# Attention logits in a one-core decoder layer: three 64-row products per half become two 128-row products, with q stacked, k doubled and padded, and three bias bands kept on chip

## The chip, the cores and the metric

The kernel runs on one core of a Trainium2 chip. The metric is device time in microseconds (us) of one execution; the median of three runs is the figure compared. The core has a matrix engine (PE, whose weight loads are listed apart as PEld), a vector engine (DVE), a scalar engine (ACT), a general engine (POOL) that also issues transfers, and a queue engine (SP) that only issues transfers.

## The reference, cut to what matters

One decoder layer over 512 tokens of width 1024, in float32. After a normalisation and one wide projection, 8 heads of differential attention run beside a recurrent branch; the two are gated, merged and followed by a squared-ReLU MLP. The part the change touches is the attention's logits:

```python
q = rmsnorm(q, q_g)                      # per head and half: 64 values
k = rmsnorm(k, k_g)
...
bias = jnp.transpose(bias_tab[rel_bucket(rel)], (2, 0, 1))
logits = jnp.einsum('bqhcd,bkhcd->bhcqk', q_blk, k) * scale   # c = 0, 1: two halves of 64
logits = logits + bias[None, :, None]
logits = jnp.where(rel >= 0, logits, -jnp.inf)
p = jax.nn.softmax(logits, axis=-1)
attn = p[:, :, 0] - lam * p[:, :, 1]
out = einsum(attn, v)
```

So each head has two logit matrices, each a product over 64 values, and the bias depends only on the head and on query minus key.

## The kernel before, in words

**Precision.** Matrix products run on a rounded float32 type. To keep accuracy each operand is split into a high part (rounded, made by ACT) and a low part (the remainder, made by DVE), and a product is three products: high by high, high by low, low by high (`mm3`, L136 to L139). Weights arrive as `wraw`, and are split into `whi` (ACT) and `wlo` (DVE), one unit of 128x1024 at a time.

**Stages.** From 0 to about 77 us the input is normalised and the first projections run. From 77 to about 283 us the attention runs; the rest of the layer follows.

**Attention.** It is one loop of 32 blocks. Block s is head s // 4 and query rows 128 * (s % 4). Per block: `logits` (PE, L563, six products of 64 rows, three for each half c; N = 256, 256, 384, 512 key columns for s % 4 = 0 to 3), `soft_a` (DVE adds the bias `toep` and takes the maximum, ACT takes the exponential), `soft_b` one step later (DVE normalises and combines the two halves; its last instruction is `pe<-pe,r`), `turn(s)` one more step later (PE transposes, L597, 128 columns each, s % 4 + 1 of them; then the split into `pt`), and `av` (PE). Between the blocks `fill_in` puts projection work for the next pair of heads on PE (products into `acc`), so that PE has something to do while the softmax of a block runs on DVE and ACT. Heads come in pairs; `qkv_pair(j)` computes q, k and v of heads 2j and 2j + 1 while pair j - 1 is in the attention loop. Its own `turn(qi, ...)` transposes q or k of one head (PE, L515, four transposes from `qn`), and `split` makes the high part (ACT, one instruction of 128x512) and the low part (DVE, one of 128x512) of `qkT`. There are 16 such turns: q and k of 8 heads.

**Bias.** `bias_table` makes for each head a 128x512 band `toep[h]` in SBUF, by two transfers on SP's queue; all eight bands have their own place.

**Order.** DVE, ACT and POOL keep the order of the program (`InOrder`). SP issues transfers in order. PE's attention instructions are placed by the compiling layer's scheduler, which may move a product past another one; its choice is fixed at build time, and the change shifts it.

Of the kernel before, what the change touches and what calls it, by code (L numbers as in the profile page):

```python
# [11 lines left out]
F32 = mybir.dt.float32  # L12
F32R = mybir.dt.float32r
I32 = mybir.dt.int32
AF = mybir.ActivationFunctionType
ALU = mybir.AluOpType
# [3 lines left out]
P = 128  # L20
S = 512
DM = 1024
NT = S // P
KT = DM // P
NH = 8
# [4 lines left out]
TW = 640  # L30
# [7 lines left out]
def tile_block(ctx: ExitStack, tc: tile.TileContext, x, w_in, w_rga, w_rgx, w_pa, w_pr, w_o,  # L38
               w_up, w_dn, rel_bias, smalls, lamv, onehot, out):
    nc = tc.nc  # L40
# [34 lines left out]
    V, A, G, T = InOrder(nc.vector), InOrder(nc.scalar), InOrder(nc.gpsimd), nc.tensor  # L75

    def psum(tag):
        return pp.tile([P, 512], F32, tag=tag, name=tag, bufs=nb[tag])
# [62 lines left out]
    def split(hi, lo, src, scale=None):  # L141
        if scale is None:
            A.copy(hi, src)
            V.tensor_tensor(out=lo, in0=src, in1=hi.bitcast(F32), op=ALU.subtract)
        else:
            A.activation(hi, src, AF.Copy, scale=scale)
            V.scalar_tensor_tensor(out=lo, in0=src, scalar=scale, in1=hi.bitcast(F32), op0=ALU.mult, op1=ALU.subtract)
# [65 lines left out]
    def rstd_of(dst, ss, n, width):  # L213
        t = sm.tile([P, width], F32, tag="ms", name="ms")
        V.tensor_scalar(out=t, in0=ss, scalar1=1.0 / n, scalar2=EPS, op0=ALU.mult, op1=ALU.add)
        G.tensor_tensor(out=dst, in0=t, in1=mhalf[:, :width], op=ALU.pow)
# [28 lines left out]
    def tok_proj(bank, ws, t):  # L245
        b = bank[:, 256 * (t % 2):256 * (t % 2) + 256]
        for k in range(KT):
            w = ws[k // 4]
            mm3(b, h_tok(k, t), (w[0][:, k % 4, :], w[1][:, k % 4, :]), k == 0, k == KT - 1)
            if t == NT - 1 and k % 4 == 3:  # L250
                wa.free()
        wa.pump()
# [42 lines left out]
    def unit(name, dt=F32R):  # L295
        return actp.tile([P, 2, S], dt, tag="unit", name=name)
# [11 lines left out]
    with tc.tile_pool(name="p1", bufs=1) as p1:  # L308
# [28 lines left out]
        ps = [[psum("at"), psum("at")] for z in range(2)]  # L337
        for k0, k1 in pieces:
            u, kk = k0 // 4, slice(k0 % 4, (k1 - 1) % 4 + 1)
# [64 lines left out]
    trep = [dp.tile([1, P * TW], F32, name=f"trep{h}", tag=f"trep{h}") for h in range(NH)]  # L404
# [3 lines left out]
    wk = es_at.enter_context(tc.tile_pool(name="wk", bufs=1, reuse_waits="tile"))  # L408
    t2 = {n: wk.tile([P, 2], F32, name=n) for n in ("ls", "le")}
    t8 = [wk.tile([P, KT], F32, name=n) for n in ("ab", "e", "den", "s", "s2", "po", "tmp", "mxl")]  # L410
    wk.tile([P, 32], F32, name="apart2")
    toep = [wk.tile([P, S], F32, tag=f"toep{h}", name=f"toep{h}") for h in range(NH)]
    PT = []
    for half in range(2):
        PT.append([wk.tile([P, 2 + 2 * half, 256], F32R, name=f"pt{half}{z}", tag=f"pt{half}{z}") for z in range(2)])
# [5 lines left out]
    def work(name):  # L421
        return wk.tile([P, S], F32, tag="pe", name=name, bufs=5)

    def bias_table():
        parts = ((0, 512), (512, 128))
        ohs = []
        for c0, n in parts:
            o = work("oh")
            nc.sync.dma_start(o[:64, :n], onehot[:, c0:c0 + n])
            ohs.append(o)  # L430
        rb = sm.tile([64, 32], F32, name="rbt", tag="rbt", bufs=1)
        G.memset(rb, 0.0)
        G.memset(rb[32:33, :], MASKED)
        nc.sync.dma_start(rb[0:NBUCKET, 0:NH], rel_bias)
        yield
        for (c0, n), o in zip(parts, ohs):
            ps = psum("at")
            T.matmul(ps[:32, :n], rb, o[:64, :n], start=True, stop=True)
            tb = work("tb")
            V.tensor_copy(tb[:32, :n], ps[:32, :n])  # L440
            nc.sync.dma_start(tdram[:, c0:c0 + n], tb[:NH, :n])
        yield
        for h in range(NH):
            nc.sync.dma_start(trep[h].rearrange("o (r y) -> o r y", r=P),
                              tdram[h:h + 1, :].rearrange("h (o y) -> h o y", o=1).broadcast_to([1, P, TW]))
            yield
            t0 = trep[h][0:1, :]
            nc.sync.dma_start(toep[h], bass.AP(tensor=t0.tensor, offset=t0.offset + 127, ap=[[TW - 1, P], [1, S]]))

    def lam_diff(lt):  # L450
        lv = lt[:, :256].rearrange("p (a b c) -> p a b c", a=2, b=2)
# [36 lines left out]
    def qkv_pair(j, qk, v):  # L488
        def proj(o, bank):
            ws = [wa.get(), wa.get()]  # L490
            for t in range(NT):
                if t % 2 == 0:
                    bank.append(psum("acc"))
                tok_proj(bank[t // 2], ws, t)
                yield 2.6

        def normed_a(b, qn):
            n = wk.tile([P, S], F32, tag="qn", name="qn", bufs=4)
            A.activation(n, b, AF.Square)
            ss = sm.tile([P, 8], F32, tag="ss8", name="ss8")  # L500
            V.tensor_reduce(out=ss, in_=n.rearrange("p (g d) -> p g d", g=8), axis=AX.X, op=ALU.add)
            rs = sm.tile([P, 8], F32, tag="rs8", name="rs8")
            rstd_of(rs, ss, 64, 8)
            qn.append(n)
            return b, n, rs

        def normed_b(b, n, rs):
            V.tensor_tensor(out=n.rearrange("p (g d) -> p g d", g=8), in0=b.rearrange("p (g d) -> p g d", g=8),
                            in1=rs.rearrange("p (g o) -> p g o", o=1).broadcast_to([P, 8, 64]), op=ALU.mult)

        def turn(qi, qn, gsc, hh):
            ps = psum("at")
            for t in range(NT):
                c0 = 256 * (t % 2) + P * hh
                T.transpose(out=ps[:, t * P:(t + 1) * P], in_=qn[t // 2][:, c0:c0 + P], identity=ident)  # L515
            d = unit("qkT")
            split(d[:, 0, :], d[:, 1, :], ps, gsc)
            qk[hh, qi] = d

        banks = {o: [] for o in (OQ, OK_, OV)}  # L520
        qn = {o: [] for o in (OQ, OK_)}
        pend, half = [], []
        for o, qi, gsc in ((OQ, 0, qg), (OK_, 1, kg), (OV, None, None)):
            for t, cost in enumerate(proj(o, banks[o])):
                half.append(None)
                ready = half.pop(0) if len(half) > 2 else None
                if ready:
                    normed_b(*ready)
                if t % 2 == 1:
                    b = banks[o][t // 2]  # L530
                    if o != OV:
                        half[-1] = normed_a(b, qn[o])
                    else:
                        vt = wk.tile([P, 2, 2, 256], F32R, tag="v", name="v", bufs=4)
                        split(vt[:, 0], vt[:, 1], b.rearrange("p (t c) -> p t c", t=2))
                        v.append(vt)
                if pend and t >= 2:
                    turn(*pend.pop(0))
                    cost += 0.45
                yield cost  # L540
                if j == 0 and o == OV and t == 0:
                    lam_diff(lt)
                if j == 0 and o != OQ:
                    next(bt)
            if o != OV:
                pend = [(qi, qn[o], gsc, 0), (qi, qn[o], gsc, 1)]

    def attention(fills, qks, vs, pads):
        st = {}

        def place(s):
            return s // NT, s % NT

        def logits(s):
            h, i = place(s)
            qk = qks[h // 2]
            qT, kT = qk[h % 2, 0], qk[h % 2, 1]
            N = max(256, P * (i + 1))
            lg = [psum("at"), psum("at")]
            for a, (x0, y0) in enumerate(((0, 0), (0, 1), (1, 0))):  # L560
                for c in range(2):
                    r = slice(64 * c, 64 * c + 64)
                    T.matmul(lg[c][:, :N], qT[r, x0, i * P:(i + 1) * P], kT[r, y0, :N], start=a == 0, stop=a == 2)  # L563
            st[s] = lg

        def soft_a(s):
# [80 lines left out]
        def at(step, f, *a):  # L647
            acts.setdefault(step, []).append((f, a))

        for s in range(NH * NT):  # L650
            h, i = place(s)
# [6 lines left out]
            if i == 3:  # L658
                at(s + 3, post_a, h)
                at(s + 4, post_b, h)  # L660
                at(s + 5, post_c, h)
                at(s + 7, post_d, h)
        order = [post_d, post_c, post_b, av, post_a, turn, logits, soft_a, soft_b]
        for step in sorted(acts):
            j = step // (2 * NT)
            if step >= 37:
# [170 lines left out]

    ga = chain(gate(tga, [3]), gate(tgr, range(4)))
    bt = bias_table()
    next(bt)  # L840
    lt = work("lt")
# [395 lines left out]
    for n, (kind, a, p, pairs) in enumerate(steps):  # L1237
# [12 lines left out]
        if kind == "pl":  # L1250
            oc, kc = int(p[1]) % 2, int(p[1]) // 2
            ps = banks[kind, a][2 * oc:2 * oc + 2]
            for m in range(8):
                u, i = (m // 4, m % 4) if kc else (m % 2, m // 2)
# [14 lines left out]
        f = FORM[p]  # L1269
        k = seen.get(o, 0)  # L1270
# [4 lines left out]
        for u in range(2):  # L1275
            d = b[u][:, :256] if isinstance(b, tuple) else b[:, 256 * u:256 * u + 256]
            for z, i in enumerate(pairs):
                for e, (l, r) in enumerate(((hi, 0), (hi, 1), (lo, 0))):
                    act = h2[:, r, i, ACT8[p]] if kind == "up" else forms[2 * a[0] + i // 2][:, r, f, i % 2]
                    I.matmul(d, l[:, i, P * u:P * u + P], act, start=p in ("M1", "M2", "M5") and k == z == e == 0 and (u == 0 or isinstance(b, tuple)),  # L1280
                             stop=i == 3 and e == 2, skip_group_check=True)
# [57 lines left out]
```

## Time and profile before

| what | value |
|---|---|
| median of 3 runs | 858.13 us (857.88 to 862.3) |
| the profiled execution's own time | 857.36 us |
| its span, first to last instruction | 855.6 us |
| outside the span | 1.8 us |
| granted PE clock | 1.00 |
| PE busy | 848.4 us, 99% of the span |
| DVE, ACT, POOL busy | 627.6, 449.2, 84.7 us |

The times are of one traced execution. PE's matrix products are pipelined, so the reported length of one (0.28 us for 256 columns) is longer than the distance from one start to the next; the distance between starts is what PE time costs, and the prediction uses that. A line number is the line of the kernel; instructions recorded by a helper all carry L67, and are told apart by the tiles they write and read.

### The profile page before, as it was taken

Reading aid. Unit: us, or ns where it says so; the run is one execution under the profiler, and the core shown is the slowest. Engines: PE = TensorE matmul, PEld = TensorE weight load, DVE = VectorE, ACT = ScalarE, POOL = GpSimd, SP = SyncE. Lnnn points to the kernel's source line nnn. Section 1 sums busy time; section 2 is a strip of 40 time slices with the busy share of each in tenths; the row PEclk is TensorE's granted clock in tenths of the full one; section 3 lists DMA queues with packets and bytes.
Section 4 is the critical chain, followed back from the end, with each engine's and each line's share of the span. In section 5 each row is a group of like instructions: output and inputs, shape, how many; then the busy total and the mean of one; then the engine's idle time right before and its main releaser. Section 6 shows DMA issues by size and latency. Waiting matters only on the chain.

```text
span 855.6 us, 13733 instructions
## 1 busy us (share of the span) xinstructions
PE 848.4 (99%) x5459; PEld 755.4 (88%) x5459; DVE 627.6 (73%) x1069; ACT 449.2 (52%) x703; POOL 84.7 (10%) x101
## 2 busy tenths in 40 slices
PE   9999999999999999999999999999999999999998
PEld 7899999999888878888878888889998998999898
DVE  6765688888765236878767767788787858776797
ACT  7444355554545225685673355654476357545642
POOL 0030222113111101111110000000000000000000
PEclk9999999999999999999999999999999999999999
DMA  5358212131231477776664461515652574456354
GB/s 201 121 167 239 90 63 86 41 110 63 76 98 38 114 226 197 207 186 190 177 176 138 117 253 50 172 25 149 204 184 57 153 241 146 125 150 196 99 143 129
DMA packets 38736, 119.76 MB, mean 140 GB/s; under 512 B 4608, under 2 KB 9416, under 8 KB 38672
## 3 DMA queue, kind: packets, MB, share of 16 engines
q1 hardware_dynamic: 31152, 92.65, 33.2%
q0 software_dynamic: 7520, 26.23, 13.6%
q8 instruction: 43, 0.70, 0.3%
q14 instruction: 21, 0.17, 0.1%
HBM read 102.05 MB, written 11.05 MB: 132 GB/s over the span
## 4 chain that ended last, share of the span: by engine, by line
PE 93%; DVE 3%; DMA 1%; ACT 1%; SPq 0%; issue 0%; DVEq 0%
PE acc L67 37%; PE acc L137 15%; PE acc L139 15%; PE acc L138 15%; PE at L563 2%; PE at L139 2%; PE at L137 2%; PE at L138 2%; DMA wraw<-in_w_in_dram 1%; DVE wlo L67 1%; PE at L597 1%; PE at L515 1%; PE at L628 1%; ACT whi L67 1%; DVE pe L67 1%; ACT pe L67 1%
## 5 line engine op out<-in xcount | busy, mean ns | idle before, releaser
L67 PE MATMUL acc<-h,whi 128*128 128x512 f32 (+1 forms) x656 | 155.7, 331 | 0.0
L67 DVE TENSOR_TENSOR wlo<-wraw,whi 128x1024 fp32r<-128x1024 f32 (+2 forms) x86 | 97.0, 1148 | 79.6 <-ACT whi L67 79.4
L67 PE MATMUL acc<-us,whi 128*128 128x256 f32 (+1 forms) x900 | 153.0, 276 | 0.0
L67 ACT CAST whi<-raw 128x1024 fp32r<-128x1024 f32 x97 | 99.7, 1049 | 87.2 <-DVE raw L67 34.1
L67 PEld LDWEIGHTS acc<-us,whi 128*128 128x128 f32 x900 | 135.7, 188 | 0.3
L67 DVE TENSOR_TENSOR wlo<-raw,whi 128x1024 fp32r<-128x1024 f32 x97 | 117.5, 1218 | 14.0 <-ACT whi L67 13.8
L67 PE MATMUL acc<-us,wlo 128*128 128x256 f32 x448 | 123.6, 276 | 0.0
L67 PEld LDWEIGHTS acc<-h,whi 128*128 128x128 f32 x656 | 110.5, 188 | 12.3
L137 PE MATMUL acc<-whi,hT 128*128 128x256 f32 x384 | 109.8, 286 | 0.0
L67 PE MATMUL acc<-h,wlo 128*128 128x256 f32 (+1 forms) x328 | 108.6, 331 | 0.0
L67 ACT CAST whi<-wraw 128x1024 fp32r<-128x1024 f32 (+2 forms) x86 | 82.6, 982 | 48.1 <-DMA wraw<-in_w_in_dram 32.9
L138 PE MATMUL acc<-wlo,hT 128*128 128x256 f32 x384 | 107.3, 280 | 0.2 <-DVE wlo L67 0.2
L67 PEld LDWEIGHTS acc<-us,wlo 128*128 128x128 f32 x448 | 84.1, 188 | 0.0
L137 PE MATMUL acc<-hT,whi 128*128 128x512 f32 x208 | 82.5, 396 | 0.7 <-ACT whi L67 0.3
L139 PE MATMUL acc<-hT,wlo 128*128 128x512 f32 x208 | 81.3, 391 | 0.7 <-DVE wlo L67 0.7
L139 PE MATMUL acc<-whi,hT 128*128 128x256 f32 x288 | 80.4, 279 | 0.0
L137 PEld LDWEIGHTS acc<-whi,hT 128*128 128x128 f32 x384 | 72.4, 188 | 4.3 <-issue 3.0
L138 PEld LDWEIGHTS acc<-wlo,hT 128*128 128x128 f32 x384 | 72.3, 188 | 1.0 <-issue 0.5
L67 ACT ACTIVATE pe<-pe,nm 128x128 f32<-128x128 f32 (+3 forms) x64 | 35.5, 556 | 66.0 <-DVE nm L67 66.0
L67 PEld LDWEIGHTS acc<-h,wlo 128*128 128x128 f32 x328 | 61.6, 188 | 6.3
L138 PE MATMUL acc<-hT,whi 128*128 128x512 f32 x156 | 60.9, 391 | 0.0
L67 POOL TENSOR_TENSOR rs<-ms,mhalf 128x8 f32<-128x8 f32 (+1 forms) x25 | 39.7, 1589 | 206.7 <-DVE ms L67 206.7
(204 smaller groups left out, 1623.9 us busy)
## 6 DMA issues: line engine op xcount, KB each, us to landing
wraw<-in_w_in_dram SPq DMA_DIRECT2D x54, 512.0 KB, 3.9
raw<-in_w_dn_dram SPq DMA_DIRECT2D x32, 512.0 KB, 4.2
raw<-in_w_up_dram SPq DMA_DIRECT2D x29, 512.0 KB, 4.0
sum<-in_w_up_dram POOLq DMA_DIRECT2D x18, 512.0 KB, 5.5
raw<-raw POOLq DMA_DIRECT2D x16, 512.0 KB, 4.6
wraw<-in_w_pa_dram SPq DMA_DIRECT2D x8, 512.0 KB, 5.5
wraw<-in_w_pr_dram SPq DMA_DIRECT2D x8, 512.0 KB, 3.8
wraw<-in_w_o_dram SPq DMA_DIRECT2D x8, 512.0 KB, 3.5
```

The source lines that it names most:

```text
L67: ins = f(*a, **k)
L137: T.matmul(o, l[0], r[0], start=first, stop=False)
L138: T.matmul(o, l[0], r[1], start=False, stop=False)
L139: T.matmul(o, l[1], r[0], start=False, stop=last)
L515: T.transpose(out=ps[:, t * P:(t + 1) * P], in_=qn[t // 2][:, c0:c0 + P], identity=ident)
L563: T.matmul(lg[c][:, :N], qT[r, x0, i * P:(i + 1) * P], kT[r, y0, :N], start=a == 0, stop=a == 2)
L597: T.transpose(out=tp[:, b * P:(b + 1) * P], in_=st[s][:, b * P:(b + 1) * P], identity=ident)
L628: T.matmul(ps[:, t:t + 1], sq[:, t * P:(t + 1) * P], ones, start=True, stop=True)
```

## The change

For each head and half c, the stationary side is now a tile of 128 rows: 64 rows hold the high part of q, the other 64 the low part of the same half. The moving side is 128 rows as well: k's high part twice (once below each half of the stack), and, in a tile `kl` of its own, k's low part over zeros. Two products then give the three terms: (high, low) of q by (high, high) of k, and (high, low) of q by (low, zero). So a block has four products of 128 rows where it had six of 64.

To make these tiles the turn's split is cut in halves of 64 rows: two ACT instructions and two DVE instructions of 64x512, where there was one each of 128x512. k's second copy of its high part is made by two transfers on POOL's queue, except for the first head of the first pair, where ACT makes it. Three `kl` tiles are rotated; POOL fills their zero rows once. The bias bands rotate through three places, so bands 3 to 7 are loaded inside the attention loop, on SP's queue.

```diff
-    toep = [wk.tile([P, S], F32, tag=f"toep{h}", name=f"toep{h}") for h in range(NH)]
+    halves = slice(0, 64), slice(64, P)
+    toep = {}
+    def toep_in(h):
+        toep[h] = wk.tile([P, S], F32, tag="toep", name="toep", bufs=3)
...
+    kl = [wk.tile([P, 2, S], F32R, tag=f"kl{n}", name=f"kl{n}") for n in range(3)]
+    for k in kl:
+        for c in range(2):
+            G.memset(k[halves[1 - c], c, :].bitcast(F32), 0.0)
...
-            d = unit("qkT")
-            split(d[:, 0, :], d[:, 1, :], ps, gsc)
-            qk[hh, qi] = d
+            d = qk[hh, qi] = unit("qkT")
+            def low(dst, c):
+                V.scalar_tensor_tensor(out=dst, in0=ps[halves[c], :], scalar=gsc[halves[c], :], in1=d[halves[c], c, :].bitcast(F32), op0=ALU.mult, op1=ALU.subtract)
+            def high(c, rows):
+                A.activation(d[rows, c, :], ps[halves[c], :], AF.Copy, scale=gsc[halves[c], :])
+            for c in range(2):
+                high(c, halves[c])
+            if qi == 0:
+                for c in range(2):
+                    low(d[halves[1 - c], c, :], c)
+            else:
+                kk = qk[hh, 2] = kl[(2 * j + hh) % 3]
+                for c in range(2):
+                    low(kk[halves[c], c, :], c)
+                for c in range(2):
+                    if j == hh == 0:
+                        high(c, halves[1 - c])
+                    else:
+                        G.dma_start(d[halves[1 - c], c, :], d[halves[c], c, :])
...
-            for a, (x0, y0) in enumerate(((0, 0), (0, 1), (1, 0))):
-                for c in range(2):
-                    r = slice(64 * c, 64 * c + 64)
-                    T.matmul(lg[c][:, :N], qT[r, x0, i * P:(i + 1) * P], kT[r, y0, :N], start=a == 0, stop=a == 2)
+            for c in range(2):
+                for z in (1, 2):
+                    T.matmul(lg[c][:, :N], qT[:, c, i * P:(i + 1) * P], qk[h % 2, z][:, c, :N], start=z == 1, stop=z == 2)
...
+        for h in range(3, NH):
+            at(NT * (h - 3) + 6, toep_in, h)
```

The scheduler also moves instructions on PE. The first place is the end of v's projection for heads 4 and 5, on PE, between the transposes of block 13 (L597, now L626) and the transposes of k of head 4 (L515, now L526); `acc_2270` here is the last tile of v's projection. Before:

```order
L597 MATMUL at_2240<-ident_73,pe_2059 128x128 x2
L563 MATMUL at_2245<-qkT_1609,qkT_1391 128x512
L563 MATMUL at_2246<-qkT_1609,qkT_1391 128x512
L563 MATMUL at_2245<-qkT_1609,qkT_1391 128x512
L563 MATMUL at_2246<-qkT_1609,qkT_1391 128x512
L563 MATMUL at_2245<-qkT_1609,qkT_1391 128x512
L563 MATMUL at_2246<-qkT_1609,qkT_1391 128x512
L137 MATMUL acc_2270<-whi_1885,hT_82 128x256
L138 MATMUL acc_2270<-wlo_1886,hT_82 128x256
```

Now, on the same engine at the same place, where `acc_2385` is already the first tile of q's projection for heads 6 and 7:

```order
L139 MATMUL acc_2271<-whi_1958,tail_83 128x256
L626 MATMUL at_2243<-ident_73,pe_2060 128x128 x2
L592 MATMUL at_2248<-qkT_1614,qkT_1392 128x512
L592 MATMUL at_2248<-kl0_486,qkT_1392 128x512
L592 MATMUL at_2249<-qkT_1614,qkT_1392 128x512
L592 MATMUL at_2249<-kl0_486,qkT_1392 128x512
L526 MATMUL at_2296<-ident_73,qn_1965 128x128 x2
L526 MATMUL at_2296<-ident_73,qn_2101 128x128 x2
L137 MATMUL acc_2385<-whi_2193,hT_82 128x256
```

Before, 24 products of v's last tile stood between block 15's logits and k's transposes; now that tile is finished ahead of block 13's transposes, and k's transposes follow the logits at once. Behind them come 5 products, head 5's k transposes, 6 products of `av`, 16 products and then the transposes of block 14.

The second place is the start of that pair's attention on PE, the first logits of head 4 (block 16). Before:

```order
L597 MATMUL at_2347<-ident_73,pe_2149 128x128 x3
L563 MATMUL at_2353<-qkT_2300,qkT_2040 128x256
L137 MATMUL acc_2378<-whi_2190,hT_82 128x256
L138 MATMUL acc_2378<-wlo_2191,hT_82 128x256
L139 MATMUL acc_2378<-whi_2190,hT_82 128x256
L563 MATMUL at_2354<-qkT_2300,qkT_2040 128x256
L563 MATMUL at_2353<-qkT_2300,qkT_2040 128x256
```

Now, on PE, the same logits:

```order
L139 MATMUL acc_2385<-whi_2223,tail_83 128x256
L592 MATMUL at_2362<-qkT_2301,qkT_2041 128x256
L592 MATMUL at_2362<-kl1_487,qkT_2041 128x256
L137 MATMUL acc_2484<-whi_2193,hT_82 128x256
L138 MATMUL acc_2484<-wlo_2194,hT_82 128x256
L139 MATMUL acc_2484<-whi_2193,hT_82 128x256
L137 MATMUL acc_2484<-whi_2193,hT_82 128x256
L592 MATMUL at_2363<-qkT_2301,qkT_2041 128x256
```

Between block 14's transposes and block 16's first logits there are now 27 products of the next pair's projection; before there was none.

The third place is POOL, around the same pair. Before:

```order
L67 TENSOR_TENSOR rs_2104<-ms,mhalf 128x8
L67 TENSOR_TENSOR rs_2235<-ms,mhalf 128x4
L67 DMA rdram<-rs_2235 128x4
L67 DMA rb<-rdram 128x512
L67 TENSOR_TENSOR rs_2443<-ms,mhalf 128x8
```

Now:

```order
L67 TENSOR_TENSOR rs_2105<-ms,mhalf 128x8
L67 TENSOR_TENSOR rs_2238<-ms,mhalf 128x4
L67 DMA rdram<-rs_2238 128x4
L67 DMA qkT<-qkT 64x512 x4
L67 DMA rb<-rdram 128x512
L67 TENSOR_TENSOR rs_2450<-ms,mhalf 128x8
```

The four copies of k stand ahead of the transfer of `rb`, which the output normalisation of an earlier head reads some steps later.

More of the change, by code (lines that the diff above doesn't have):

```diff
@@ L411, in tile_block @@
     wk.tile([P, 32], F32, name="apart2")
-    toep = [wk.tile([P, S], F32, tag=f"toep{h}", name=f"toep{h}") for h in range(NH)]
+    halves = slice(0, 64), slice(64, P)
+    toep = {}
+    def toep_in(h):
+        toep[h] = wk.tile([P, S], F32, tag="toep", name="toep", bufs=3)
+        t0 = trep[h][0:1, :]
+        nc.sync.dma_start(toep[h], bass.AP(tensor=t0.tensor, offset=t0.offset + 127, ap=[[TW - 1, P], [1, S]]))
+    kl = [wk.tile([P, 2, S], F32R, tag=f"kl{n}", name=f"kl{n}") for n in range(3)]
+    for k in kl:
+        for c in range(2):
+            G.memset(k[halves[1 - c], c, :].bitcast(F32), 0.0)
     PT = []
@@ L446, in bias_table @@
             yield
-            t0 = trep[h][0:1, :]
-            nc.sync.dma_start(toep[h], bass.AP(tensor=t0.tensor, offset=t0.offset + 127, ap=[[TW - 1, P], [1, S]]))
+            if h < 3:
+                toep_in(h)
     def lam_diff(lt):
@@ L556, in logits @@
             qk = qks[h // 2]
-            qT, kT = qk[h % 2, 0], qk[h % 2, 1]
+            qT = qk[h % 2, 0]
             N = max(256, P * (i + 1))
             lg = [psum("at"), psum("at")]
-            for a, (x0, y0) in enumerate(((0, 0), (0, 1), (1, 0))):
-                for c in range(2):
-                    r = slice(64 * c, 64 * c + 64)
-                    T.matmul(lg[c][:, :N], qT[r, x0, i * P:(i + 1) * P], kT[r, y0, :N], start=a == 0, stop=a == 2)
+            for c in range(2):
+                for z in (1, 2):
+                    T.matmul(lg[c][:, :N], qT[:, c, i * P:(i + 1) * P], qk[h % 2, z][:, c, :N], start=z == 1, stop=z == 2)
             st[s] = lg
@@ L662, in attention @@
                 at(s + 7, post_d, h)
-        order = [post_d, post_c, post_b, av, post_a, turn, logits, soft_a, soft_b]
+        for h in range(3, NH):
+            at(NT * (h - 3) + 6, toep_in, h)
+        order = [toep_in, post_d, post_c, post_b, av, post_a, turn, logits, soft_a, soft_b]
         for step in sorted(acts):
```

## The prediction

> **What bounds the kernel now.** I read first the busy shares and the chain that ended last, then the busy time by stage, then the attention's instructions in order of time.
>
> ```profile
> PE 848.4 (99%) x5459; PEld 755.4 (88%) x5459; DVE 627.6 (73%) x1069; ACT 449.2 (52%) x703; POOL 84.7 (10%) x101
> PE 93%; DVE 3%; DMA 1%; ACT 1%; SPq 0%; issue 0%; DVEq 0%
> ```
>
> PE is busy 99% of the span and makes 93% of the chain: a PE microsecond saved anywhere is a microsecond, as long as PE doesn't start to wait. The view by stretches says where it could (span, then busy time of PE, PEld, DVE, ACT, POOL):
>
> ```profile
> 30.00:55.00 25.00, 24.85 (x169) 22.72 (x167) 21.30 (x35) 15.87 (x22) 2.45 (x7) 1.00 0.44 139
> 127.00:176.40 49.40, 49.40 (x411) 45.98 (x410) 41.09 (x119) 26.22 (x62) 12.24 (x11) 1.00 0.25 76
> 176.40:227.40 51.00, 50.79 (x425) 47.21 (x424) 42.19 (x120) 27.08 (x64) 11.67 (x10) 1.00 0.23 73
> 310.00:855.60 545.60, 541.33 (x3310) 483.44 (x3310) 411.61 (x531) 294.63 (x384) 32.26 (x43) 1.00 0.53 156
> ```
>
> The second and third rows are one pair of heads each. PE is full, but DVE is at 83%: 8 to 9 us of DVE idle per pair is all the room there is. After 310 us the change touches nothing and PE is full (541.33 of 545.60): what is won or lost by then reaches the end unchanged.
>
> **The change part by part: the logits on PE.** A block's cost is read from starts, since a product's reported length overlaps the next. The rows are a block of 256 columns, one of 512, and for comparison two transposes with no logits behind them:
>
> ```profile
> 76.84 0.60 PE L515 MATMUL at<-ident,qn 128*128 128x128 f32 x4
> 77.37 0.62 PE L563 MATMUL at<-qkT 64*128 64x256 f32 x6
> ...
> 78.14 0.29 PE L138 MATMUL acc<-wlo,hT 128*128 128x256 f32 x1
> ...
> 118.37 0.38 PE L597 MATMUL at<-ident,pe 128*128 128x128 f32 x2
> 118.68 0.96 PE L563 MATMUL at<-qkT 64*128 64x512 f32 x6
> ...
> 119.80 0.28 PE L137 MATMUL acc<-whi,hT 128*128 128x256 f32 x1
> ...
> 120.51 0.38 PE L515 MATMUL at<-ident,qn 128*128 128x128 f32 x2
> ...
> 120.85 0.28 PE L138 MATMUL acc<-wlo,hT 128*128 128x256 f32 x1
> ```
>
> Two transposes and one full product take 120.85 - 120.51 = 0.34 us; with four transposes that is 0.56 (0.11 each). With the 512 block between them it is 119.80 - 118.37 = 1.43, so the block costs 1.09; with the 256 block 78.14 - 76.84 = 1.30, so 0.74. The pace of full products of 256 and 512 columns is the distance of far starts by their count:
>
> ```profile
> 169.05 0.28 PE L138 MATMUL acc<-wlo,hT 128*128 128x256 f32 x1
> ...
> 171.55 0.28 PE L139 MATMUL acc<-whi,tail 128*128 128x256 f32 x1
> ...
> 270.58 0.40 PE L137 MATMUL acc<-hT,whi 128*128 128x512 f32 x1
> ...
> 272.86 0.39 PE L138 MATMUL acc<-hT,whi 128*128 128x512 f32 x1
> ```
>
> 2.50 us over 22 steps is 0.114, and 2.28 over 10 is 0.228. Six 64-row products run as three pairs side by side, so in slots alone the old blocks are 3 x 0.114 = 0.34 and 3 x 0.228 = 0.68; the other 0.40 is waiting on the way into and out of the 64-row form. The new blocks are four full products with the same shape as their neighbours: 0.456 and 0.912. Saved: 0.28 and 0.18, and for 384 columns, which lie between, 0.24. Over 16, 8 and 8 blocks: 4.5 + 1.4 + 1.9 = 7.8; I take 8.0, since the trace's rounding is 0.01 per block.
>
> [...]
>
> Two old blocks, the first of a pair, are cut in one and five with products between, and pay the entrance twice. From the chain:
>
> ```profile
> 176.49 0.31 PE at L563
> 176.80 0.32 PE acc L137
> ```
>
> The lone product and the one behind it take 0.63 instead of 0.06 + 0.11: 0.45 more, twice: 0.9 saved, since the new blocks can be cut at no cost.
>
> **The extra work on DVE and ACT.** Each of 16 turns issues two instructions of 64x512 where one of 128x512 stood. Half the rows don't make it shorter, by these two rows (32 rows by 512, the maximum, and 128 by 512):
>
> ```profile
> L67 DVE COPY tb<-at x2: 268/474/680, 56.2 to 56.8; 32x512 f32<-32x512 f32 x1, 32x128 f32<-32x128 f32 x1
> L67 DVE COPY rb<-acc x1: 690/690/690, 27.4 to 27.4; 128x512 f32<-128x512 f32 x1
> ```
>
> So a turn costs 0.75 more on DVE and 0.67 more on ACT (the `qkT` row of ACT below), 12 us and 11 us in all, and two more ACT copies (1.3) at the first head. Four turns lie before 79 us, beside a DVE that is half idle. Twelve lie in the three pairs: 3 us of DVE each, in 8 to 9 us of idle time. That fits in sum, not everywhere.
>
> **Where PE will wait.** The stretch from block 13's transposes to block 14's, PE, DVE and ACT in turn:
>
> ```profile
> 167.59 0.41 PE L597 MATMUL at<-ident,pe 128*128 128x128 f32 x2
> 171.66 0.49 PE L515 MATMUL at<-ident,qn 128*128 128x128 f32 x3
> 176.00 0.49 PE L597 MATMUL at<-ident,pe 128*128 128x128 f32 x3
> ...
> 166.96 0.48 DVE L67 SCALAR_TENSOR_TENSOR pe<-pe,r 128x256 f32<-128x256 f32 x1
> 168.66 2.36 DVE L67 TENSOR_TENSOR wlo<-wraw,whi 128x1024 fp32r<-128x1024 f32 x2 [1.14 <-ACT whi L67]
> 170.94 0.68 DVE L67 TENSOR_TENSOR qn<-acc,rs 128x512 f32<-128x512 f32 x1
> 174.71 0.62 DVE L67 SCALAR_TENSOR_TENSOR pe<-pe,r 128x384 f32<-128x384 f32 x1
> ...
> 160.31 0.67 ACT L67 ACTIVATE qkT<-at,qg 128x512 fp32r<-128x512 f32 x1
> 167.59 1.98 ACT L67 CAST whi<-wraw 128x1024 fp32r<-128x1024 f32 x2
> 175.50 0.67 ACT L67 ACTIVATE qkT<-at,smt 128x512 fp32r<-128x512 f32 x1
> ```
>
> Block 13's softmax ends at 167.44 and PE transposes it at 167.59. DVE then waits for two weight casts, makes `wlo` twice, `qn` (which k's transposes read, end 171.62) and ends block 14's softmax at 175.33: 7.9 us during which PE had 8.4 us of work. By the new order PE has, between the same two transposes, 2 transposes, 0.91 of logits, 8 transposes of k and 27 products: 0.22 + 0.91 + 0.88 + 3.1 = 5.1 us. So PE waits up to 2.8 us, at k's transposes. The seven products moved ahead of block 13 make PE later there by 0.8, and the turn of q just before makes DVE later by 0.75; these cancel, and what is left is how late PE already is, so the wait is 1.6 to 2.8; I take 2.2, the middle. The same order stands in the next pair: 4.4 for both. In the first pair k's transposes keep 12 products ahead of the second two: 0.4.
>
> The last pair has such a place too. There block 31's logits are followed by 6 `av` and 3 products before block 30's transposes:
>
> ```profile
> 268.80 0.38 PE L597 MATMUL at<-ident,pe 128*128 128x128 f32 x2
> ...
> 272.30 0.62 DVE L67 SCALAR_TENSOR_TENSOR pe<-pe,r 128x384 f32<-128x384 f32 x1
> ```
>
> Softmax 30 ends 4.1 us after block 29's transposes start; PE has 0.22 + 0.91 + 0.68 + 0.68 = 2.5. Wait 1.6, less what PE is late: 1.4. For blocks 1 and 3, where transposes follow their softmax with no slack and PE comes 0.5 us earlier: 0.9.
>
> **The copies, memsets and bands.** k's second copy waits for ACT, then for POOL to issue. Nearest rows, both on POOL's queue:
>
> ```profile
> rb<-rdram POOLq DMA_DIRECT2D x8, 256.0 KB, 3.6
> rdram<-rs POOLq DMA_DIRECT2D x8, 2.0 KB, 2.0
> ...
> DMA to landing us min/median/max: 3.5/3.6/5.0
> ```
>
> For 128 KB between these I take 2.8, with 2.0 and 5.0 as ends. ACT's half is done at 175.50 + 0.67, 0.84 after softmax 14; a copy issued at 0.95 lands at 3.75. PE comes to block 16's logits 0.15 + 0.33 + 27 x 0.114 = 3.56 after that softmax: wait 0.2 per pair, 0.6 for three (0 to 2.4 each). Queued behind the copies on POOL is `rb`, with its normalisation some steps later, and the next `rs`; I cost both at nothing, hidden by the step or more between. If they come late, DVE is late next. The six memsets:
>
> ```profile
> L67 POOL MEMSET pt<- x4: 204/204/206, 43.4 to 43.8; 128x128 f32 x4
> ```
>
> At four times the columns at most 0.82 each, 4.9 us on a POOL that was busy 2.45 of 25 us (30 to 55). The bands' late loads stand on SP's queue behind casts long done; each weighs 256 KB where a DMA share of 0.25 leaves room: nothing, or 0.3 if one delays a weight load.
>
> [...]
>
> **The sum.** -8.0 - 0.9 + 4.4 + 0.4 + 1.4 + 0.9 + 0.6 = -1.2, on the profiled execution's own 857.36 (span 855.6 and 1.8 around it). That execution stands 0.8 below the median of 858.13, so on the median: 856.9.
>
> **The rivals.** *The new waits don't come*, because PE reaches those places late, or DVE's chain was waiting for PE and moves with it. For: in the old order PE waited hardly at all (49.40 busy of 49.40). Against: the 7.9 us are DVE and ACT instructions in a row. With half of the 7.1 of waits: 853.4; with none and no copy waits: 849.2.
>
> *The copies are late.* Place: the first logits of heads 2, 4 and 6. Each microsecond of landing beyond 2.8 is a microsecond of PE, three times; it gives slower by over 0.5% from a landing of 4.6 us on. At 5.5: 856.9 + 3 x 2.7 = 865.0. For: POOL's in-order queue and the landing of 5.0 in the worst row. Against: the medians of 2.0 and 3.6.
>
> *The waiting around the logits stays*, as a property of this place and not of the 64 rows. Then each block has four slots for three: 16 x 0.114 + 8 x 0.17 + 8 x 0.228 = 5.0 more and none of the 8.9 saved: 858.1 + 5.0 + 7.7 = 870.8. Against it stands the 0.34 row.
>
> **How the numbers follow.** About 0.5% (4.3 us) is what a measurement of this kernel can tell from no change. My sum 0.45, half or none of the waits 0.37 (most of it beyond 0.5%), late copies 0.12, waiting stays 0.02; 0.04 for a DVE that pays its 9 us. The likeliest time is 856.9, its own range 854 to 860. For 8 in 10 I take 850.5, near the low end of the first rival, to 861.5, a copy landing of 4.3. Faster 0.37, same 0.46, slower 0.17.
>
> **What would show it.** Right: 64-row products gone and block starts 0.46 and 0.91 apart with no 0.2 entrance; PE idle of about 2 us at k's transposes (L526) near 170 and 220 us, put down to DVE; `qkT` on ACT and DVE at 0.67 and 0.75 for 64 rows; copies landing in about 2.8. Wrong: no idle at L526; idle at L592 put down to a DMA; 64-row ACT or DVE instructions at half the time, which would take the sum down with the chain; or DVE's idle per pair well under 5 us.

## The result: slower by 0.9%, with waits on PE where the work of DVE and ACT has grown

| what | before | after |
|---|---|---|
| median | 859.12 us (858.13 at the prediction) | 867.25 us (864.15 to 868.5) |
| ratio to the kernel before, 95% interval | | 1.0088 (1.0067 to 1.0109) |
| the profiled execution's own time, its span | 857.36, 855.6 us | 864.15, 862.4 us |
| first logits; transposes of block 31 | 77.37; 278.63 us | 78.12; 288.51 us |

The changed kernel is about 8 us slower. Its first logits come 0.75 us later, the transposes of the last block 9.9 us later. The busy shares and the shares of the chain that ended last:

```profile
PE 845.4 (98%) x5395; PEld 760.4 (88%) x5395; DVE 640.3 (74%) x1085; ACT 462.2 (54%) x721; POOL 95.3 (11%) x121
PE 81%; DVE 8%; ACT 6%; DMA 3%; issue 2%; SPq 0%; ACTq 0%
```

PE's part of the chain has gone from 93% to 81%; DVE and ACT now make 14%, from 4%. By stretches (span, then busy time of PE, PEld, DVE, ACT, POOL; PE's clock; DMA): two pairs of heads, from the transposes of block 11 to those of block 27, then the stretch around PE's longest wait, cut in three:

```profile
159.70:267.02 107.32, 100.66 (x709) 92.57 (x707) 85.87 (x232) 58.05 (x130) 22.22 (x25) 0.98 0.31 87
...
175.44:178.85 3.41, 1.24 (x12) 1.24 (x12) 3.41 (x7) 0.81 (x3) 0.55 (x1) 1.00 0.58 168
178.85:182.27 3.42, 3.42 (x19) 3.42 (x17) 2.39 (x10) 2.24 (x6) 1.06 (x2) 0.50 0.66 214
182.27:185.68 3.41, 3.41 (x31) 3.41 (x31) 2.77 (x4) 2.98 (x5) 2.09 (x5) 1.00 0.46 94
```

The same two pairs of the kernel before:

```profile
155.96:255.80 99.84, 99.63 (x750) 89.08 (x749) 79.34 (x224) 52.57 (x122) 17.96 (x17) 1.00 0.25 77
```

Two pairs took 7.5 us longer. PE, full before, was idle for 6.7 of them; DVE was busy 6.5 more and ACT 5.5 more. What PE waited for between 77 and 290 us (total, times, longest):

```profile
PE at L526 <- DVE qn L67: 5.6, 4, 2.5
PE at L657 <- ACT osq L67: 1.7, 3, 0.8
PE at L626 <- DVE pe L67: 1.3, 1, 1.3
PE at L592 <- ACT qkT L67: 0.3, 1, 0.3
```

By the distances of starts, which also hold the waits of a few tenths, it is 12.3 us, against 0.8 before. The longest wait, on PE from the transposes of block 13 on (start, duration, instruction, count; in brackets the idle time ahead of it and what ended it):

```profile
173.53 0.41 PE L626 MATMUL at<-ident,pe 128*128 128x128 f32 x2
173.69 0.48 PE L592 MATMUL at<-qkT 128*128 128x512 f32 x1
174.01 0.39 PE L592 MATMUL at<-kl,qkT 128*128 128x512 f32 x1
174.24 0.39 PE L592 MATMUL at<-qkT 128*128 128x512 f32 x1
174.46 0.39 PE L592 MATMUL at<-kl,qkT 128*128 128x512 f32 x1
174.69 0.38 PE L526 MATMUL at<-ident,qn 128*128 128x128 f32 x2
177.61 0.44 PE L526 MATMUL at<-ident,qn 128*128 128x128 f32 x2 [2.54 <-DVE qn L67]
...
179.40 0.41 PE L139 MATMUL at<-pt,v 128*128 128x256 f32 x1
179.62 0.41 PE L137 MATMUL at<-pt,v 128*128 128x256 f32 x1
```

The logits are what was forecast: starts 0.22 to 0.23 apart from the second on, and no wait at the entrance (174.01 - 173.53 = 0.48 us for two transposes and the first product, where 0.45 is the usual pace). Behind them k's third transpose stands for 2.5 us until DVE has made `qn`. Then PE's starts are 0.21 to 0.22 apart where 0.114 is usual: the 0.50 in the clock column of the stretch from 178.85 us.

Why `qn` is late stands in the chain that ended last, in order of time (start, us, what):

```profile
158.79 0.57 ACT qkT L67
159.37 0.69 ACT qkT L67
160.09 0.74 DVE qkT L67
160.85 0.77 DVE qkT L67
161.64 0.69 DVE pt L67
...
163.25 1.09 ACT pe L67 x4
164.34 0.48 ACT qn L67
164.82 0.57 ACT qkT L67
165.41 0.69 ACT qkT L67
166.12 0.74 DVE qkT L67
166.88 0.76 DVE qkT L67
167.67 1.11 DVE of L67
168.81 0.73 ACT aT L67
...
176.87 0.69 DVE qn L67
177.61 0.44 PE at L526 x2
```

In these 19 us, and in the 18 us before them, no instruction of PE is in the chain: DVE and ACT hand work to each other. Both q turns of the pair are in it, each with all four of its halves in a row, because DVE's first half starts only when both of ACT's are done (166.12 behind 165.41 + 0.69). A turn is 2.8 us of this chain; with one instruction per engine it would be 0.67 + 0.75 = 1.4.

### The profile page after: what moved, and what is told of

Its sections match the earlier page's. It is cut to its first block, busy times and chain, and to the rows that moved or that the text cites. A ratio compares the mean times of both kernels' runs of the same rounds, so it can differ in the third digit from the quotient of the medians.

```text
span 862.4 us, 13719 instructions
## 1 busy us (share of the span) xinstructions
PE 845.4 (98%) x5395; PEld 760.4 (88%) x5395; DVE 640.3 (74%) x1085; ACT 462.2 (54%) x721; POOL 95.3 (11%) x121
## 4 chain that ended last, share of the span: by engine, by line
PE 81%; DVE 8%; ACT 6%; DMA 3%; issue 2%; SPq 0%; ACTq 0%
PE acc L67 35%; PE acc L139 13%; PE acc L137 13%; PE acc L138 13%; DVE wlo L67 2%; ACT pe L67 2%; DVE pe L67 2%; PE at L137 2%; ACT whi L67 2%; PE at L138 1%; PE at L139 1%; PE at L592 1%; ACT qkT L67 1%; DMA wraw<-in_w_in_dram 1%; DVE qkT L67 1%
## 5 line engine op out<-in xcount | busy, mean ns | idle before, releaser
L67 DVE TENSOR_TENSOR wlo<-raw,whi 128x1024 fp32r<-128x1024 f32 x97 | 117.6, 1219 | 17.2 <-ACT whi L67 17.1
L67 PEld LDWEIGHTS acc<-h,whi 128*128 128x128 f32 x656 | 110.4, 188 | 12.3
```

Source lines behind the costliest of these rows:

```text
L67: ins = f(*a, **k)
```

## The experiments

**The two parts of the change, each alone.** Theory (work): the doubled halves on ACT and DVE make PE wait. Rivals: the moved PE order does (order), or DVE can't follow a shorter PE whatever the split costs (pace). First with PE held to the order in which the program writes its products:

```diff
+    pinned.append(1)       # T is then InOrder(nc.tensor)
     attention(...)
+    pinned.clear()
```

> The kernel before, with PE's products held to the order in which the program writes them, from the start of the attention to its end. In the trace of before the scheduler's order was nearly the written one, so both theories say: as before, 859 (857 to 862). It is the base of the three other runs with PE held in written order. Work theory (the two halves of 64 rows on ACT and DVE make PE wait): 859. Order theory (the moved PE order makes PE wait): 859.

> The changed kernel with the logits' four 128-row products kept, PE held in written order, and the turn's split as it was before: one ACT and one DVE instruction of 128x512, no copies by POOL. Left out: the stacking of q and doubling of k, so the logits sum both halves. Work theory: the whole gain comes, 859 less 8 to 9 = 850 to 851, and waits of PE between 77 and 283 us of under 3 us in sum. Order theory: the written order keeps 24 products ahead of k's transposes, so no waits, the same 850 to 851. If instead the faster logits alone outrun DVE (a third theory, DVE as the bound of a pair), 854 to 858.

> The kernel before with its six 64-row products per block, PE held in written order, and only the turn's split cut in two halves of 64 rows on ACT and on DVE, as in the change. Work theory: 1.4 us per turn in series on ACT and DVE, of which PE must wait for a part at each of 12 turns: 863 to 870. Order theory: without the moved order DVE has its slack, 859 to 862.

> The changed kernel in full, PE held in written order during the attention (24 products of v's last tile again ahead of k's transposes). Work theory: DVE's chain is what PE waits for, so the wait only moves to block 14's and 30's transposes: 863 to 868. Order theory: the 2.7 us waits at k's transposes go, and with them the halved clock behind them: 852 to 856.

Measured: 863.24 (1.0055, 1.0034 to 1.0076); 858.21; 872.91; 872.26. All four lie above what I had expected (858.21 by 0.2), since their base does: the written order costs 0.55% by itself. PE then waits 1.4 us for the softmax in front of the transposes of each of blocks 3, 11 and 19; the scheduler's order hides these. Against that base the logits alone gain 5.0 and the halves alone cost 9.7, and with both the kernel is 9.0 slower. The written order brings no gain, so the moved order alone is not the cause: with 24 products again ahead of k's transposes, PE waits in front of block transposes instead (1.3 us each at blocks 13 and 21 in `change_in_order`, none there in `before_in_order`). This order also makes k's copies late (PE waited 4.9 us in six places for `qkT<-qkT`), which muddies the last of the four. So the parts again, in the order that the scheduler chooses for each:

```diff
# logits_alone
...
+            split(d[:, 0, :], d[:, 1, :], ps, gsc)
...
+                    T.matmul(lg[c][:, :N], ..., qk[h % 2, 1][:, z - 1, :N], ...)
# split_alone: the kernel before, with
-            split(d[:, 0, :], d[:, 1, :], ps, gsc)
+            for c in range(2):
+                A.activation(d[r, 0, :], ps[r, :], ...)       # r: 64 rows
+            for c in range(2):
+                V.scalar_tensor_tensor(out=d[r, 1, :], ...)
```

> The changed kernel with the four 128-row products kept, but the turn's split as before (one ACT and one DVE instruction of 128x512, no copies by POOL), PE in the order that the scheduler chooses for it. Left out: the stacking of q and the doubling of k, so the logits sum both halves. With PE in written order this part alone gave 5.0 (863.2 to 858.2), because two microseconds of wait stood at each odd head's last block. Work theory (the doubled halves on ACT and DVE are what PE waits for): the scheduler's order hides those waits as it does in the kernel before, so 850 to 853 and under 3 us of waits. Pace theory (DVE's softmax chain can't follow a PE that is 8 us shorter, whatever the split costs): 855 to 858.

> The kernel before with its six 64-row products, and only the turn's split cut in two halves of 64 rows on ACT and on DVE; PE in the order that the scheduler chooses. In written order this part cost 9.7. Work theory: 864 to 870, with waits at the places of the changed kernel (k's transposes, the ones sums). Pace theory: as long as PE is not shortened DVE has its slack, 859 to 862.

Measured: 853.70 (ratio 0.9923, 0.9899 to 0.9947) and 867.90 (1.0097, 1.0071 to 1.0123), beside 859.96 for the kernel before. The first lies 0.7 above the work theory's range and below the pace theory's, the second inside the work theory's. The gain of the logits is there, 6.3 us, bands and zero rows included, which this kernel has. The halves alone cost 8, as much as the whole change: with them in, the 6.3 us that the logits save on PE are gone. The two pairs of `split_alone`, and then of `logits_alone`, say so:

```profile
161.41:268.40 106.99, 103.24 (x742) 89.62 (x741) 85.89 (x232) 57.93 (x129) 18.00 (x17) 1.00 0.22 72
```

```profile
156.23:254.52 98.29, 97.50 (x714) 91.34 (x713) 78.30 (x223) 52.20 (x122) 17.99 (x17) 1.00 0.26 83
```

With halves two pairs take 107 us with the old logits (106.99) and with the new (107.32). The order isn't the same in these kernels: between the first two and the last two transposes of k of head 4 the scheduler put 22 products in `logits_alone`, 4 in `split_alone` and none in the changed kernel. The cost of the halves in one fixed order is the 9.7 above.

**Which engine's halves.** The kernel before, with one engine's instruction cut and the other's whole (the diff is half of the last one):

> The kernel before, with only ACT's high part of each turn cut in two halves of 64 rows (0.67 us more per turn); DVE's low part is one instruction of 128x512 as before. With both engines' halves the kernel took 867.9, 8 more. Series theory (DVE's low part waits for both of ACT's halves, so ACT's extra 0.67 and DVE's extra 0.75 add up on one chain): nearly half of the 8, 862.5 to 865. DVE theory (only DVE's busy time counts, ACT has room): 859 to 861.

> The kernel before, with only DVE's low part of each turn cut in two halves of 64 rows (0.75 us more per turn); ACT's high part is one instruction of 128x512 as before. Series theory: a little over half of the 8, 863 to 865. DVE theory: nearly all of the 8, 865.5 to 868.

Measured: 861.08 (1.0021, 1.0006 to 1.0037) and 863.45 (1.0054, 1.0035 to 1.0074). DVE's halves weigh more, and neither theory fits both: the series theory has DVE's number and missed ACT's, the DVE theory comes near ACT's and missed DVE's. By the medians 1.6 and 4.0 make 5.6, and both together cost 7.9. A little slack that the first addition uses up would give this; the slack itself was not measured.

**Undoing the halves by transfers.** q's turn is split in whole tiles again, and transfers on POOL's queue place the pieces; then also k's turn of the odd heads:

```diff
+            if j and (qi == 0 or hh):        # q_by_copies: j and qi == 0
+                split(d[:, 0, :], qlo, ps, gsc)
+                G.dma_start(d[halves[1], 1, :], d[halves[1], 0, :])
+                if qi == 0:
+                    G.dma_start(d[halves[0], 1, :], qlo[halves[1], :])
+                    later.append((d[halves[1], 0, :], qlo[halves[0], :]))
...
```

> The changed kernel, but q's turns of heads 2 to 7 split as before (one ACT and one DVE instruction of 128x512) and three transfers on POOL's queue then bring the halves to their places; two bias bands instead of three make room for the low part's tile. k's turns stay in halves. Series theory: q's turns are the ones in front of the odd heads' softmax (blocks 11 to 13), where two thirds of the loss arose, so 860.5 to 863.5, with the 2.7 us waits near 1.3. Rival (k's turns are the place, q's have slack): 865.5 to 868. Second rival (transfers of 128 KB late or POOL's queue blocked by the third, which waits for the first): over 868.

> As with q's copies, and k's turn of each odd head (3, 5, 7) too: one ACT and one DVE instruction of 128x512, and five transfers on POOL's queue; its logits come four blocks later. Only k's turn of heads 2, 4, 6 and the first pair keep the halves. Series theory: three of four turns cost what they did before, so 857.5 to 861. Rival (POOL's queue of 13 transfers per pair holds up the inverse roots that it also makes, and with them DVE): 863 to 870.

Measured: 864.57 (1.0062, 1.0043 to 1.0082) and 858.98 (0.9999, 0.9981 to 1.0018). With three of four turns in heads 2 to 7 whole, the kernel is back at the level of the kernel before. It is still 5.3 above `logits_alone`, of which the quarter of the halves that is left would make some 2 (an estimate from the 8 of `split_alone`); the rest is not explained. The first version gained less than expected. One line of its DVE shows a part of it:

```profile
219.16 0.75 DVE L67 SCALAR_TENSOR_TENSOR qlo<-at,qg,qkT 128x512 fp32r<-128x512 f32 x1 [2.52 <-DMA qkT<-qlo]
```

Head 7's q turn waited 2.5 us until the single `qlo` tile had been read by a transfer (0.4 in the second version). PE also ran at half its clock for 6.8 us of this profile before the end (mean granted clock 0.996, and 1.000 in the second version). What each makes of the 5.6 us between the two versions was not measured. In the second version PE's waits are half of those of the changed kernel (L675 are its `ones` sums, products with a column of ones that sum the squares `osq` of a head's output; L644 its block transposes):

```profile
PE at L526 <- DVE qn L67: 1.8, 3, 0.9
PE at L675 <- ACT osq L67: 1.6, 2, 0.8
PE at L644 <- DVE pe L67: 0.6, 1, 0.6
```

**The halved clock.** Products that no one reads fill the wait:

```diff
+                if qi and j > 1 and hh == 0 and t == 2:
+                    for _ in range(14):
+                        T.matmul(ps[:, 256:512], hT[0][:, 0, :P], hT[0][:, 0, :256], ...)
```

> The changed kernel with 14 products of 256 columns (into the unused half of the transposes' own bank, 1.6 us) put in front of the third transpose of k of heads 4 and 6, where PE waits 2.7 us. They delay nothing as long as the wait is over 1.6. Clock theory (a long wait also halves PE's clock for one stretch of 3.413 us in some executions): 863.5 to 866, and no halved stretch near 180 and 232 us. Without such a cost: as the changed kernel, 866.5 to 868.

Measured: 868.29 (1.0095, 1.0075 to 1.0116). The wait was filled as meant, and no stretch of this profile before the end had half the clock (mean granted clock 0.999):

```profile
174.37 1.91 PE L527 MATMUL at<-hT 128*128 128x256 f32 x14
177.15 0.44 PE L529 MATMUL at<-ident,qn 128*128 128x128 f32 x2 [0.86 <-DVE qn L67]
```

But the time did not fall, and the clock theory's 863.5 to 866 was missed. `split_alone`, too, lost its 8 us with no halved stretch before its end (0.999). In these kernels the halved clock came with some of the waits, and nothing showed that their time hangs on it.

**Other orders.** Four kernels move work without changing any of it: `qn` a tile earlier, turns earlier by a wider fill (with the kernel before as control), and the heads' closing work later.

```diff
-                ready = half.pop(0) if len(half) > 2 else None      # qn_one_tile_early
+                ready = half.pop(0) if len(half) > 1 else None
-    attention(..., [3.6] * 4 + [2.8])                               # wider_fill
+    attention(..., [4.0] * 4 + [2.8])
+            late = [z for z in todo if z[0] in (post_d, post_a) and step < 36]
...
             fill_in(...)                                            # post_behind_fill
+            for f, a in late:
+                f(*a)
```

> The changed kernel with q's and k's normalisation (qn) put one tile of the projection earlier on DVE, so one of the two weight casts (1.2 us) stands behind it instead of ahead. Work theory: the wait at k's transposes of heads 4 and 6 falls from 2.7 to about 1.5 and part of it appears at the ones sums and the next blocks' transposes: 863 to 866. If the waits come from somewhere else than DVE's queue ahead of qn: 867 to 868.

> The changed kernel, all its instructions kept, with 4.0 instead of 3.6 us of projection work asked for between two blocks, so that q's and k's turns come one to two blocks earlier and the work left over at a pair's end is spread over its blocks. Place theory (the doubled halves cost because they stand on DVE right ahead of an odd head's softmax, while DVE is idle elsewhere): 858 to 863. Amount theory (the 12 + 11 us of extra work on DVE and ACT have no room at any place, whatever the order): 866 to 869.

> The kernel before with the same 4.0 instead of 3.6: the control for the run with wider fill. PE is full in it already, so both theories say 857.5 to 861 (before: 859.4).

> The changed kernel, with an even or odd head's closing work (post_a: two ACT copies of o; post_d: DVE's of, then aT on ACT and DVE; 3.6 us on the chain) put behind the projection work of its step instead of ahead of the block's transposes and softmax. All instructions are kept. Chain theory (from block 10 to k's transposes the chain of DVE and ACT is longer than PE's work, so whatever leaves it is won): the chain ahead of k's transposes loses 3.6 per pair, less what comes back at block 14: 857 to 863. If the amount of work on DVE alone counts: 866 to 869.

Measured: 873.31, 876.88, 858.63 and 880.65. All three on the changed kernel missed: they made it slower, by 1.5%, 2.0% and 2.4% over the kernel before, while the control did not move (0.9998, 0.9974 to 1.0022). In the last one the wait at k's transposes of head 4 did go, but the scheduler now put 80 projection products between the transposes of blocks 12 and 13, and these waited for `qn` themselves:

```profile
PE acc L137 <- DVE qn L67: 6.2, 3, 3.0
PE at L657 <- ACT osq L67: 3.1, 3, 2.1
PE at L526 <- DVE qn L67: 2.7, 3, 1.8
```

In these three profiles PE ran at half its clock for 17.1, 13.7 and 13.7 us before the end, against 3.4 in the changed kernel (mean granted clock 0.989, 0.992 and 0.992, against 0.998). So up to half of these times may be the clock's share of the loss; the runs don't separate it from the order's. It isn't settled what the best order would be, and a place with room for the halves was not found. The same moves on the version by copies:

> The version with q's and the odd heads' k by copies (858.98), with 4.0 instead of 3.6. Place theory: its remaining waits (6.0, at k's transposes and the ones sums) shrink to 2 to 3: 854 to 857. Amount theory: three quarters of the extra work are already gone, so its waits are those of the order alone: 857 to 860.

> The version with q's and the odd heads' k by copies, with the weight cast of a projection tile put behind the normalisation instead of ahead of it, so that k's qn stands behind one low weight part (1.2 us) on DVE and not two. Place theory: the waits at k's transposes (0.75 and 1.1) go, 856 to 858.5. Amount theory: nothing changes, 858 to 860. In the changed kernel a similar move (qn a tile early) made it 6 slower, by waiting on the inverse root; if that comes back: over 861.

> The version with q's and the odd heads' k by copies (858.98), with the closing work behind the projection work as well. Chain theory: its 1.8 at k's transposes and 2.1 at the ones sums go, a wait of up to 1 per pair at block 14 comes: 855 to 858, faster than the kernel before. If the closing work is late for block 14: 859 to 861.

Measured: 867.86, 861.29 (1.0017, 1.0000 to 1.0034) and 869.41: none better than 858.98. The first and the last lie above everything expected of them, the first with no halved stretch before its end (mean granted clock 0.999). In the second no wait was listed at k's transposes any more, as the place theory had it, but the time did not fall. No complete version beat the kernel before.

**What the runs say together.** Two pairs (transposes of block 11 to 27) of the kernels in the order that the scheduler and the program gave them, by the view of stretches:

| kernel | time | two pairs | DVE busy | share | ACT busy |
|---|---|---|---|---|---|
| logits alone | 853.70 | 98.29 | 78.30 | 80% | 52.20 |
| before | 859.12 | 99.84 | 79.34 | 79% | 52.57 |
| ACT's halves alone | 861.08 | 100.87 | 79.31 | 79% | 58.23 |
| q and odd k by copies | 858.98 | 101.72 | 80.57 | 79% | 53.87 |
| DVE's halves alone | 863.45 | 104.75 | 84.74 | 81% | 52.63 |
| q by copies | 864.57 | 105.35 | 82.03 | 78% | 55.56 |
| both halves alone | 867.90 | 106.99 | 85.89 | 80% | 57.93 |
| changed kernel | 867.25 | 107.32 | 85.87 | 80% | 58.05 |

DVE is busy 79 to 81% of the two pairs in seven of the eight, and 78% in q by copies; in the three kernels with moved work it is busy less (76%, 74% and 78% for wider fill, closing work behind the fill and early `qn`). The length follows DVE's work more than ACT's: 5.4 us more on DVE came with 4.9 us more length, 5.7 us more on ACT with 1.0. I read it so, without a run that tests it: the kernel before stands close to two limits at once, PE (99.63 of 99.84 us) and the chain of DVE and ACT, so that a longer chain makes PE wait at once.

The lengths are not a measure of PE's work, since the scheduler moves projection products into and out of the stretch. In `logits_alone` it holds 17 more of them of 512 columns and 21 fewer of 256 than before, at 0.228 and 0.114 us each 1.5 us more, and PE is busy 97.50 of 98.29. So the 1.6 us by which it is shorter than before are not all that a shorter PE gains, and the limit by the chain shows only where the chain got longer.

## Why the prediction was wrong, point by point

**The logits: right.** Full products at full pace and no entrance; 8.0 and 0.9 were forecast; alone they gained 6.3 (4.6 to 8.7 by the interval), with 1.9 us of waits of PE left in that kernel, 1.1 more than before: some 7.4 by this estimate. From the transposes at 173.53 to the next ones at 174.69, two transposes and the four products take 1.16 us, where 2 x 0.11 + 4 x 0.228 make 1.13; in the kernel before, the block of 512 columns with its neighbours held some 0.40 more than its slots.

**Durations of the halves: right.** 0.66 to 0.69 on ACT, 0.73 to 0.76 on DVE, for 64 rows.

**Room for them: the step that failed.** "3 us of DVE each, in 8 to 9 us of idle time. That fits in sum" took DVE's idle time for room. Most of it was time in which DVE waited for ACT's part of the same piece of work. In the two pairs of the kernel before, DVE was idle for 20.5 us, and these waits make 17.3 of them:

```profile
DVE wlo L67 <- ACT whi L67: 7.6, 7, 2.2
DVE pt L67 <- ACT pt L67: 5.0, 9, 0.8
DVE aT L67 <- ACT aT L67: 3.2, 4, 0.8
DVE qkT L67 <- ACT qkT L67: 1.5, 2, 0.8
```

In the changed kernel, with 6.5 us more work on DVE, its waits for ACT are still 17.0, and the idle share is still a fifth. The doubled halves cost 8 alone, an outcome to which the prediction had given 0.04, as "a DVE that pays its 9 us".

**"These cancel": the same error at one place.** The turn of q ahead of block 13 was taken to make DVE later by 0.75. It is 1.4 by the chain above, since ACT's half goes in series too, and the chain holds two such turns, from 158.79 and from 164.82. In the trace of before, softmax 12 to softmax 13 took 7.75 us (159.69 to 167.44); after it took 9.27 (164.11 to 173.38).

**Where PE waits.** Blocks 14 and 22, at k's transposes: 2.2 each taken, 2.7 each measured, near the upper bound of 2.8: the 2.2 assumed that PE would be late at block 13, but it transposed that block 0.15 behind its softmax (173.53 and 173.38). First pair: 0.4 and 0.9. Block 30: 1.4 and 1.4. Blocks 1 and 3: 0.9 and nothing. Copies: 0.6 and nothing at heads 2, 4 and 6; they landed in 2.2 to 2.5 us, 2.3 in the median, where 2.8 was taken:

```profile
qkT<-qkT POOLq DMA_DIRECT2D x14, 128.0 KB, 2.3
```

Not foreseen: 2.6 at the `ones` sums (L657), where ACT's `osq` is late in the same chain, 0.5 at the first logits, 0.7 at the transposes of other blocks, and the halved clock, some 1.4 (14 steps of 0.1). The forecast of the waits was 7.7, the measured growth 11.5, in which the wait at the first logits is counted. 11.5 + 1.4 - 8.9 makes 4.0 of the 6.8 by which the profiled executions differ; 2.8 are not assigned. With the 7.4 of `logits_alone` in place of 8.9 it would be 1.3.

**The rivals.** Waits that don't come, late copies and waiting that stays at the logits: none happened. Two of them had a slower kernel in their prices (865.0 and 870.8), but for reasons that the trace doesn't show; the reason that it does show was in the 0.04 at the end.

## What to carry to other kernels

Before you take the idle time of a helper engine for room, look at what ended each gap. Where it is another helper, working for the first one's own next step, the gap can move along with the work, as DVE's did here. Cutting an instruction by rows doubled its time here (64 rows took 0.68 us on ACT and 0.75 on DVE, 128 rows 0.67 and 0.75). Where the consumer waits for the whole tile, both engines' extra times add up at that place: a turn took 2.8 us of the chain instead of 1.4. Over the whole kernel much of it stays hidden, 8 us of the some 23 that were added on the two engines, so the cost has to be read along the chain and not from either engine's busy time. When PE and such a chain are both near full, a saving on PE that adds to the chain can turn into waits on PE.

## What was not expected of the hardware

A wait of PE was followed by a slower clock. In the changed kernel PE was idle for 2.2 us of the stretch from 175.44 us, and its clock was 0.50 for the next 3.41 us. The idle time alone did not tell where this happened. Here, in `change_in_order`, PE was busy 2.12 of 3.41 us, and the clock was halved in the next stretch:

```profile
226.30:229.71 3.41, 2.12 (x17) 1.93 (x16) 2.17 (x11) 2.32 (x6) 0.00 (x0) 1.00 0.02 5
229.71:233.12 3.41, 3.41 (x18) 3.31 (x17) 3.41 (x4) 1.62 (x3) 0.00 (x0) 0.50 0.32 112
```

And here, in the changed kernel, PE was busy only 1.60 of 3.41 and kept its clock, behind a wait of 2.51 us where the one ahead of the halved stretch was 2.54:

```profile
230.05:233.46 3.41, 1.60 (x11) 1.42 (x12) 3.41 (x9) 0.46 (x2) 0.91 (x1) 1.00 0.69 183
233.46:236.88 3.42, 3.42 (x21) 2.91 (x21) 2.11 (x9) 2.59 (x6) 0.93 (x3) 1.00 0.32 125
```

What decides it is not shown by these runs.
